# A depthwise convolution on VectorE: seven stored phases instead of four, and a layer norm two units later

## The chip, the cores and the metric

The kernel runs on one core of a Trainium2 chip. The metric is the device time of one execution in microseconds, from the start of the program to its end, taken over several runs of the same kernel; beside it stands one profiled execution, from which all the rows below come.

## The reference

A decoder trunk of two layers over 512 positions of 1024 channels (batch 1, float32). Layer 0 mixes tokens by a gated DeltaNet; layer 1, which the change touches, by a convolution module. Both layers then attend to a memory of 256 rows and apply a squared-ReLU MLP. The module of layer 1:

```python
def causal_depthwise_conv(x, w):
    """x (B, S, C), w (W, C); out[t] = sum_j w[j] * x[t - (W-1) + j] (left zero padding)."""

def conformer_conv(h, w_pw1, b_pw1, w_dw, b_dw, ln_g, ln_b, w_pw2, b_pw2):
    u = h @ w_pw1 + b_pw1
    u = u[..., :D_MODEL] * jax.nn.sigmoid(u[..., D_MODEL:])
    c = causal_depthwise_conv(u, w_dw) + b_dw
    c = jax.nn.silu(layer_norm(c, ln_g, ln_b))
    return c @ w_pw2 + b_pw2
```

The depthwise convolution has 31 taps per channel. Beside this module the kernel computes, in the same stage, the keys and values of layer 1's memory attention (`mem_h @ w_kv`), which depend on nothing in it.

## The kernel before

Activations lie transposed in SBUF: a tile is 128 channels by 512 positions, and 1024 channels are eight tiles, m = 0 to 7. In layer 1 the positions are kept in phases: column 128 r + i of a tile is position 4 i + r, so a tile is four phases of 128.

**Weights.** Every matrix arrives in half tiles of 128 x 1024. SyncE issues the load (`raw`, L193), ScalarE rounds it to the high half (`wh`, L204), VectorE subtracts for the low half (`wl`, L72), and each product is three matmuls: high by high, low by high, high by low (L220 to L222; L251 to L253 where the activation is the stationary side). The loads run up to four half tiles ahead, the splits three (`NW`). The third matmul of a unit is the first that needs `wl`.

**The stage.** `conformer` runs 32 units in the order of `CONV_SEQ`: 16 units "p" of the first projection (two for each channel tile, the value and the gate), then 16 units "k" of keys and values (eight for K, eight for V). After each unit, extra work is placed by hand in `CONV_AFTER`, as pairs of unit index and step:

- ("t", m): GpSimd builds the nine tap tiles of channel tile m (`taps`), for the convolution on TensorE.
- ("c", m, j...): convolution of column blocks j of tile m as matmuls with the tap tiles. Tiles 3 to 7 go this way; their gated input is first spread by 16 DMAs on SyncE into `xg`.
- ("d", m): for tiles 0 to 2 (`NDVE` is 3) the convolution is done on VectorE. "d" transposes the finished sum on TensorE (`cvT`) and adds it to the rows `cy` with their statistics.
- ("l", 0): layer norm over channels: aggregate, root, and eight normalisations on VectorE.
- ("o", m): transpose back, silu, and split of tile m, input to the final projection that follows unit 31.

**Taps on VectorE.** `pw_ev(m)` makes the gated input and, for m below 3, writes it into `xg`: four phases of 136 columns, of which the first 8 are zero. The tap with delay d, written as d = 4 u + e, adds to output phase r the input phase r - e shifted by u columns if r is at least e, and phase r + 4 - e shifted by u + 1 otherwise. So a tap with e = 0 is one instruction of 4 x 128 columns, and any other is two, of (4 - e) x 128 and e x 128 columns. The tap d = 0 runs on ScalarE and starts the sum `ca`. The tap instructions wait in a list, `todo`; after each unit and each convolution step `taps_dve(us)` issues `us * TAP_RATE` of them:

```python
            taps_dve(5.4 if kind == "p" else 2.8)
            for what, m, *js in after.pop(i, ()):
                {"t": taps, "c": lambda m: conv(m, js), "l": lambda m: ln(), "o": ln_out, "d": turn}[what](m)
                taps_dve({"c": 2.0 * len(js)}.get(what, 0.0))
```

The framework's scheduler orders the instructions of each engine and sets the semaphores; buffers come from pools and are reused in turn. The `cv` pool, from which `xg` comes, has six buffers for eight tiles; the `fs` pool has three buffers of 128 x 1024, which are otherwise used in layer 0 and at the very end.

Of the kernel before, what the change touches and what calls it, by code (L numbers as in the profile page):

```python
# [8 lines left out]
F32 = mybir.dt.float32  # L9
F32R = mybir.dt.float32r  # L10
AF = mybir.ActivationFunctionType
ALU = mybir.AluOpType
AX = mybir.AxisListType

P = 128
NT = 512
NDVE = 3
# [23 lines left out]
def tile_trunk(ctx, tc, xT, memT, prm_d, adt_d, bdw_d, w_ab, w_kq, w_v, w_z, w_dno, w_pw1, w_pw2,  # L41
               w_q, w_k, w_vv, w_o, w_up, w_dn, yT):
    nc = tc.nc
    pe, act, dve, pool = nc.tensor, nc.scalar, nc.vector, nc.gpsimd
# [3 lines left out]
    fsp = ctx.enter_context(tc.tile_pool(name="fsp", bufs=3))  # L48
# [6 lines left out]
    def nm(s):  # L55
        cnt[0] += 1
        return f"{s}_{cnt[0]}"

    def slot(dt=F32, s="u", shape=(P, NT)):
        return up.tile(list(shape), dt, tag="u", name=nm(s))  # L60
# [10 lines left out]
    def tt(e, o, a, b, op):  # L71
        e.tensor_tensor(out=o, in0=a, in1=b, op=op)  # L72

    def stt(o, a, s, b, op0, op1):
        dve.scalar_tensor_tensor(out=o, in0=a, scalar=s, in1=b, op0=op0, op1=op1)  # L75
# [7 lines left out]
    def c4(t):  # L83
        return t.rearrange("p (c i) -> p c i", c=4)
# [9 lines left out]
    def pc(name, i=0):  # L94
        return prm[:, OFF[name] + i:OFF[name] + i + 1]
# [67 lines left out]
    for kind, gq in DN_ORDER:  # L163
        for i in range(2):
            j = gq * 2 + i
            src = {"k": w_kq[gq * 4 + i], "q": w_kq[gq * 4 + 2 + i], "z": w_z[j], "v": w_v[j]}[kind]
# [781 lines left out]
    def conformer(norm, hres, nxt):  # L948
# [12 lines left out]
        def pw_ev(m):  # L961
            sg = slot(s="sg")
            tt(dve, sg, st.pop((m, 1)), norm.rb, ALU.mult)
            act.activation(sg, sg, AF.Sigmoid, bias=pc("b_pw1", 8 + m))
            a = slot(s="pa")
            tt(dve, a, st.pop((m, 0)), norm.rb, ALU.mult)
            x = wp.tile([P, 544], F32, tag="cv", name=nm("xg"), bufs=NCV)
            x4 = c4(x)
            pool.memset(x4[:, :, 0:8], 0.0)
            if m < NDVE:  # L970
                stt(x4[:, :, 8:136], c4(a), pc("b_pw1", m), c4(sg), ALU.add, ALU.mult)
                todo.extend(dve_conv(m, x4))
                return
            gl = slot(s="glu")
            stt(gl, a, pc("b_pw1", m), sg, ALU.add, ALU.mult)
            for j in range(4):
                for b in range(4):
                    nc.sync.dma_start(out=x4[32 * b:32 * b + 32, j, 8:136],
                                      in_=gl[32 * j:32 * j + 32, 128 * b:128 * b + 128])
            xg[m] = x4  # L980

        todo, acc = [], {}

        def dve_conv(m, x4):

            def tap(a, d, r0, r1, u):
                w = pc("w_tap", m * 31 + 30 - d)
                src = x4[:, (r0 - d) % 4:(r0 - d) % 4 + r1 - r0, 8 - u:136 - u]
                if d == 0:
                    act.activation(a[:, r0:r1, :], src, AF.Copy, scale=w)  # L990
                else:
                    stt(a[:, r0:r1, :], src, w, a[:, r0:r1, :], ALU.mult, ALU.add)

            acc[m] = slot(s="ca")
            for d in range(31):
                u, e = divmod(d, 4)
                yield lambda d=d, e=e, u=u: tap(c4(acc[m]), d, e, 4, u)
                if e:
                    yield lambda d=d, e=e, u=u: tap(c4(acc[m]), d, 0, e, u + 1)

        def taps_dve(us):
            for _ in range(min(len(todo), round(us * TAP_RATE))):
                todo.pop(0)()
# [60 lines left out]
        for i, (kind, u) in enumerate(CONV_SEQ):  # L1064
            if kind == "p":
                m, hf = divmod(u, 2)
                pw_mm(m, hf)
                if (m, hf) == (0, 0):
                    norm.stat()
                if (m, hf) == (1, 0):  # L1070
                    norm.spread()
                    pw_ev(0)
                if hf == 1 and m > 0:
                    pw_ev(m)
            else:
                kv_unit(1, u)
# [4 lines that stand above are left out]
# [84 lines left out]
    for gq in range(2):  # L1165
# [6 lines left out]
        for i in range(4):  # L1172
            h = 4 * gq + i
            m = MG[gq] + i * MSTEP[gq] // 2
# [34 lines left out]
    def do_w(m):  # L1209
        return wnext(("do", m // 2), m % 2), psum("do")  # L1210
# [11 lines left out]
    for m in range(2, 8):  # L1222
        w, ps = do_w(m)
# [52 lines left out]
    def out_half(half, prev):  # L1276
# [8 lines left out]
        for t in range(KT):  # L1285
# [3 lines left out]
            if t in OUT:  # L1289
# [30 lines left out]
REC = (39, 68)  # L1320
MEM = 53
MLP_ORDER = [("up", 0), ("up", 1), ("dn", 0), ("up", 2), ("dn", 1), ("up", 3), ("dn", 2), ("dn", 3)]
TAP_RATE = 1.5
CONV_SEQ = [("p", i) for i in range(16)] + [("k", i) for i in range(16)]
CONV_AFTER = [(3, ("t", 4)), (9, ("c", 3, 0, 1)), (11, ("c", 3, 2, 3)), (11, ("t", 5)), (12, ("c", 4, 0, 1)),
              (13, ("c", 4, 2, 3)), (13, ("t", 6)), (14, ("c", 5, 0, 1, 2, 3)), (14, ("t", 7)), (15, ("d", 0)),
              (16, ("c", 6, 0, 1, 2, 3)), (17, ("d", 1)), (18, ("c", 7, 0, 1, 2, 3)), (18, ("d", 2)), (18, ("l", 0))]
CONV_AFTER += [(23 + _m, ("o", _m)) for _m in range(8)]


def _tiles_a(np, w):
# [87 lines left out]
```

## Time and profile before

| | |
|---|---|
| median of 3 runs | 1600.11 us (1599.11 to 1601.5) |
| the profiled execution | 1601.85 us, of which the span of the program's instructions is 1599.7 |
| granted TensorE clock, mean | 0.983 of full speed |
| TensorE busy | 1542.7 us (96%) |
| VectorE busy | 924.3 us (58%) |
| ScalarE busy | 660.6 us (41%) |
| GpSimd busy | 275.9 us (17%) |
| chain that ended last | TensorE 89%, VectorE 3%, GpSimd 3%, ScalarE 2% |

Times in the profile are microseconds from the start of the span unless marked ns. A group of instructions is given by its line, engine, operation, and output and input tiles by the program's names, then the count, the busy time, the mean of one in ns, and the idle time of the engine before them with what ended it. Matmuls overlap, so a matmul's duration is longer than the distance between two starts; this holds in a small way for VectorE too.

### The profile page before, as it was taken

Reading aid. Unit: us, or ns where it says so; the run is one execution under the profiler, and the core shown is the slowest. Engines: PE = TensorE matmul, PEld = TensorE weight load, DVE = VectorE, ACT = ScalarE, POOL = GpSimd, SP = SyncE. Lnnn points to the kernel's source line nnn. Section 1 sums busy time; section 2 is a strip of 40 time slices with the busy share of each in tenths; the row PEclk is TensorE's granted clock in tenths of the full one; section 3 lists DMA queues with packets and bytes.
Section 4 is the critical chain, followed back from the end, with each engine's and each line's share of the span. In section 5 each row is a group of like instructions: output and inputs, shape, how many; then the busy total and the mean of one; then the engine's idle time right before and its main releaser. Section 6 shows DMA issues by size and latency. Waiting matters only on the chain.

```text
span 1599.7 us, 20039 instructions
## 1 busy us (share of the span) xinstructions
PE 1542.7 (96%) x7864; PEld 1307.5 (82%) x7864; DVE 924.3 (58%) x1373; ACT 660.6 (41%) x1011; POOL 275.9 (17%) x314
## 2 busy tenths in 40 slices
PE   9998997899999999999999999799999999999997
PEld 6777885798888888888888889788888888888897
DVE  6886878576455444343436599974545443444443
ACT  6656573745444433232314321173434442322332
POOL 1526334502111100000111308102012000000002
PEclk9999999899999999999999999899999999999999
DMA  5221112153211232232232421253213222322321
GB/s 178 67 72 60 53 51 95 53 172 110 94 63 64 92 105 93 94 104 92 94 104 93 141 90 47 85 160 106 79 40 99 95 97 92 105 93 93 104 93 53
DMA packets 47614, 147.09 MB, mean 92 GB/s; under 512 B 6304, under 2 KB 11040, under 8 KB 47520
## 3 DMA queue, kind: packets, MB, share of 16 engines
q1 hardware_dynamic: 47520, 145.81, 27.6%
q8 instruction: 62, 1.02, 0.3%
q14 instruction: 32, 0.26, 0.1%
HBM read 142.38 MB, written 2.10 MB: 90 GB/s over the span
## 4 chain that ended last, share of the span: by engine, by line
PE 89%; DVE 3%; POOL 3%; ACT 2%; issue 1%; DMA 0%; DVEq 0%; SPq 0%; POOLq 0%; ACTq 0%
PE dn L222 7%; PE dn L220 7%; PE dn L221 7%; PE up L220 7%; PE up L222 7%; PE up L221 7%; PE pw L220 3%; PE pw L221 3%; PE pw L222 3%; PE q L220 2%; PE xo L221 2%; PE q L221 2%; PE q L222 2%; PE cv L1024 2%; PE xo L220 2%; PE xo L222 2%
## 5 line engine op out<-in xcount | busy, mean ns | idle before, releaser
L204 ACT CAST wh<-raw 128x1024 fp32r<-128x1024 f32 x248 | 260.5, 1051 | 717.5 <-PE dn L221 191.4
L72 DVE TENSOR_TENSOR wl<-raw,wh 128x1024 fp32r<-128x1024 f32 x248 | 314.2, 1268 | 127.4 <-ACT wh L204 121.5
L220 PE MATMUL up<-xh,wh 128*128 128x512 f32 x512 | 200.2, 391 | 0.0
L222 PE MATMUL up<-xh,wl 128*128 128x512 f32 x512 | 199.2, 389 | 0.0
L221 PE MATMUL up<-xl,wh 128*128 128x512 f32 x512 | 199.2, 389 | 0.0
L220 PE MATMUL dn<-uh,wh 128*128 128x512 f32 x448 | 174.3, 389 | 0.0
L221 PE MATMUL dn<-ul,wh 128*128 128x512 f32 x448 | 174.3, 389 | 0.0
L222 PE MATMUL dn<-uh,wl 128*128 128x512 f32 x448 | 174.3, 389 | 0.0
L72 DVE TENSOR_TENSOR h<-dn,h 128x512 f32<-128x512 f32 x56 | 41.8, 747 | 170.4 <-PE dn L222 170.4
L75 DVE SCALAR_TENSOR_TENSOR rl<-up,rb 128x512 f32<-128x512 f32 x64 | 44.2, 691 | 156.9 <-PE up L222 156.9
L221 PEld LDWEIGHTS up<-xl,wh 128*128 128x128 f32 x512 | 96.1, 188 | 20.3 <-issue 0.5
L220 PEld LDWEIGHTS up<-xh,wh 128*128 128x128 f32 x512 | 96.1, 188 | 20.1 <-issue 0.5
L222 PEld LDWEIGHTS up<-xh,wl 128*128 128x128 f32 x512 | 96.1, 188 | 20.1
L72 POOL TENSOR_TENSOR tap<-ident,prm 128x512 f32<-128x512 f32 x45 | 61.0, 1388 | 278.6 <-PE up L222 263.8
L221 PEld LDWEIGHTS dn<-ul,wh 128*128 128x128 f32 x448 | 84.1, 188 | 17.6
L222 PEld LDWEIGHTS dn<-uh,wl 128*128 128x128 f32 x448 | 84.1, 188 | 17.5
L220 PEld LDWEIGHTS dn<-uh,wh 128*128 128x128 f32 x448 | 84.1, 188 | 17.3
L72 POOL TENSOR_TENSOR sq<-sq,sq 128x512 f32<-128x512 f32 x30 | 49.9, 1664 | 255.4 <-ACT sq L295 167.7
L75 DVE SCALAR_TENSOR_TENSOR ca<-xg,prm,ca 128x384 f32<-128x384 f32 (+3 forms) x159 | 88.2, 607 | 0.3
L220 PE MATMUL h<-xh,wh 128*128 128x512 f32 x192 | 77.5, 403 | 1.3 <-ACT xh L288 1.3
L221 PE MATMUL h<-xl,wh 128*128 128x512 f32 x192 | 75.5, 393 | 0.6 <-DVE xl L75 0.6
L222 PE MATMUL h<-xh,wl 128*128 128x512 f32 x192 | 75.2, 392 | 0.0
(320 smaller groups left out, 3204.4 us busy)
## 6 DMA issues: line engine op xcount, KB each, us to landing
raw<-w_up SPq DMA_DIRECT2D x64, 512.0 KB, 3.5
raw<-w_dn SPq DMA_DIRECT2D x64, 512.0 KB, 3.5
raw<-w_pw SPq DMA_DIRECT2D x24, 512.0 KB, 3.7
raw<-w_kq SPq DMA_DIRECT2D x16, 512.0 KB, 3.6
raw<-w_k SPq DMA_DIRECT2D x16, 512.0 KB, 3.7
raw<-w_vv SPq DMA_DIRECT2D x16, 512.0 KB, 4.0
raw<-w_q SPq DMA_DIRECT2D x16, 512.0 KB, 3.6
raw<-w_o SPq DMA_DIRECT2D x16, 512.0 KB, 3.6
```

Of the source, the lines that this page charges most:

```text
L72: e.tensor_tensor(out=o, in0=a, in1=b, op=op)
L75: dve.scalar_tensor_tensor(out=o, in0=a, scalar=s, in1=b, op0=op0, op1=op1)
L204: act.copy(h, raw)
L220: pe.matmul(ps, wh, xh, start=first, stop=False)
L221: pe.matmul(ps, wh, xl, start=False, stop=False)
L222: pe.matmul(ps, wl, xh, start=False, stop=last)
L1024: pe.matmul(o, x, TAPS[m][2 * j + u // 4][:, (u % 4) * P:(u % 4 + 1) * P], start=u == 0, stop=False)
```

## The change

For tiles 0 to 2 the gated input is now kept in seven phases of 144 columns in one `fs` buffer, `x7`. Phases 3 to 6 are the four phases as before, at column 8; phases 0 to 2 are copies of phases 4 to 6, shifted by one column, made by one ScalarE copy of 3 x 128 columns. Then output phases 0 to 3 of the tap (u, e) read the stored phases 3 - e to 6 - e, all with the same shift u, and every tap is one instruction of 4 x 128 columns. There are 93 tap instructions instead of 162, three of them on ScalarE as before. The zeros are 7 x 10 columns, set by GpSimd.

`TAP_RATE` goes from 1.5 to 0.75 instructions per microsecond of a step. The transposes of tile 2 and layer norm move from unit 18 to unit 20, and the eight outputs of layer norm each one unit later, the last now after unit 31. Tiles 3 to 7 keep their `xg` buffers.

```diff
--- before.py
+++ after.py
@@ -964,13 +964,16 @@
             act.activation(sg, sg, AF.Sigmoid, bias=pc("b_pw1", 8 + m))
             a = slot(s="pa")
             tt(dve, a, st.pop((m, 0)), norm.rb, ALU.mult)
+            if m < NDVE:
+                x7 = fsp.tile([P, 1024], F32, tag="fs", name=nm("x7"))[:, 0:1008].rearrange("p (q t) -> p q t", q=7)
+                pool.memset(x7[:, :, 0:10], 0.0)
+                stt(x7[:, 3:7, 8:136], c4(a), pc("b_pw1", m), c4(sg), ALU.add, ALU.mult)
+                act.copy(x7[:, 0:3, 9:137], x7[:, 4:7, 8:136])
+                todo.extend(dve_conv(m, x7))
+                return
             x = wp.tile([P, 544], F32, tag="cv", name=nm("xg"), bufs=NCV)
             x4 = c4(x)
             pool.memset(x4[:, :, 0:8], 0.0)
-            if m < NDVE:
-                stt(x4[:, :, 8:136], c4(a), pc("b_pw1", m), c4(sg), ALU.add, ALU.mult)
-                todo.extend(dve_conv(m, x4))
-                return
             gl = slot(s="glu")
             stt(gl, a, pc("b_pw1", m), sg, ALU.add, ALU.mult)
             for j in range(4):
@@ -981,22 +984,19 @@
 
         todo, acc = [], {}
 
-        def dve_conv(m, x4):
-
-            def tap(a, d, r0, r1, u):
-                w = pc("w_tap", m * 31 + 30 - d)
-                src = x4[:, (r0 - d) % 4:(r0 - d) % 4 + r1 - r0, 8 - u:136 - u]
+        def dve_conv(m, x7):
+
+            a = acc[m] = slot(s="ca")
+
+            def tap(d):
+                w, u, e = pc("w_tap", m * 31 + 30 - d), d // 4, d % 4
+                src = x7[:, 3 - e:7 - e, 8 - u:136 - u]
                 if d == 0:
-                    act.activation(a[:, r0:r1, :], src, AF.Copy, scale=w)
+                    act.activation(c4(a), src, AF.Copy, scale=w)
                 else:
-                    stt(a[:, r0:r1, :], src, w, a[:, r0:r1, :], ALU.mult, ALU.add)
-
-            acc[m] = slot(s="ca")
-            for d in range(31):
-                u, e = divmod(d, 4)
-                yield lambda d=d, e=e, u=u: tap(c4(acc[m]), d, e, 4, u)
-                if e:
-                    yield lambda d=d, e=e, u=u: tap(c4(acc[m]), d, 0, e, u + 1)
+                    stt(c4(a), src, w, c4(a), ALU.mult, ALU.add)
+
+            return [lambda d=d: tap(d) for d in range(31)]
 
         def taps_dve(us):
             for _ in range(min(len(todo), round(us * TAP_RATE))):
@@ -1320,12 +1320,12 @@
 REC = (39, 68)
 MEM = 53
 MLP_ORDER = [("up", 0), ("up", 1), ("dn", 0), ("up", 2), ("dn", 1), ("up", 3), ("dn", 2), ("dn", 3)]
-TAP_RATE = 1.5
+TAP_RATE = 0.75
 CONV_SEQ = [("p", i) for i in range(16)] + [("k", i) for i in range(16)]
 CONV_AFTER = [(3, ("t", 4)), (9, ("c", 3, 0, 1)), (11, ("c", 3, 2, 3)), (11, ("t", 5)), (12, ("c", 4, 0, 1)),
               (13, ("c", 4, 2, 3)), (13, ("t", 6)), (14, ("c", 5, 0, 1, 2, 3)), (14, ("t", 7)), (15, ("d", 0)),
-              (16, ("c", 6, 0, 1, 2, 3)), (17, ("d", 1)), (18, ("c", 7, 0, 1, 2, 3)), (18, ("d", 2)), (18, ("l", 0))]
-CONV_AFTER += [(23 + _m, ("o", _m)) for _m in range(8)]
+              (16, ("c", 6, 0, 1, 2, 3)), (17, ("d", 1)), (18, ("c", 7, 0, 1, 2, 3)), (20, ("d", 2)), (20, ("l", 0))]
+CONV_AFTER += [(24 + _m, ("o", _m)) for _m in range(8)]
 
 
 def _tiles_a(np, w):
```

## The prediction

> **What bounds the kernel now.** I read the page first (busy shares, slices, chain), then the stretches of 10 us around the conformer, then the groups by form, then the order in time of VectorE, GpSimd, SyncE and TensorE.
>
> ```profile
> span 1599.7 us, 20039 instructions
> PE 1542.7 (96%) x7864; PEld 1307.5 (82%) x7864; DVE 924.3 (58%) x1373; ACT 660.6 (41%) x1011; POOL 275.9 (17%) x314
> PE   9998997899999999999999999799999999999997
> DVE  6886878576455444343436599974545443444443
> PEclk9999999899999999999999999899999999999999
> ```
>
> TensorE is the bound nearly everywhere. Slices are 40 us wide; counted from 0, slice 25 (1000 to 1040 us) has TensorE at 7 and the clock at 8, while VectorE is at 9 in slices 23 to 25. That is the conformer. Cut finer (columns: PE, PEld, DVE, ACT, POOL busy, granted clock, DMA share, GB/s):
>
> ```profile
> 1000.00:1010.00 10.00, 10.00 (x91) 10.00 (x90) 9.93 (x22) 0.00 (x0) 4.15 (x4) 1.00 0.30 107
> 1010.00:1020.00 10.00, 1.27 (x11) 1.07 (x10) 9.93 (x23) 3.08 (x4) 0.00 (x0) 0.70 0.02 5
> 1020.00:1030.00 10.00, 7.03 (x43) 7.03 (x44) 10.00 (x29) 0.00 (x0) 0.00 (x0) 0.62 0.18 43
> ...
> 1010.44 0.60 PE L1008 MATMUL cvT<-ident,ca 128*128 128x128 f32 x4
> 1022.97 0.58 PE L222 MATMUL K<-mh,wl 128*128 128x256 f32 x1 [11.70 <-DVE wl L72]
> ...
> 1021.71 1.21 DVE L72 TENSOR_TENSOR wl<-raw,wh 128x1024 fp32r<-128x1024 f32 x1
> ```
>
> There is one stall in the conformer: 11.7 us before the third matmul of K unit 2. It waits for that unit's low half `wl`, a VectorE subtraction that starts at 1021.71, because VectorE, busy 9.93 us of every 10 here, is behind with its queue. So the stage's price is VectorE's queue ahead of this `wl`.
>
> **A second price, the clock.** After the stall TensorE is slow for a while. Third matmuls of neighbouring K triples, before and after it:
>
> ```profile
> 1008.51 0.28 PE L222 MATMUL K<-mh,wl 128*128 128x256 f32 x1
> 1008.87 0.28 PE L222 MATMUL K<-mh,wl 128*128 128x256 f32 x1
> ...
> 1023.78 0.41 PE L222 MATMUL K<-mh,wl 128*128 128x256 f32 x1
> 1024.42 0.41 PE L222 MATMUL K<-mh,wl 128*128 128x256 f32 x1
> ```
>
> A triple takes 0.64 us instead of 0.36; over seven triples that is 2.0 us. Stall and slow clock together: 13.7 us, the most that the change can win here. The Trainium skill (TensorE: Matmul & The Clock Gate, Part 1) says that the clock halves after an idle window of about 3.4 us and returns after as long a busy one; the granted 0.70 and 0.62 in the rows agree. By it, waits of 1 or 2 us, such as I expect below, leave the clock alone.
>
> **Fewer tap instructions.** Before, a tap whose shift is a multiple of four is one instruction of 512 columns; every other tap is two (384 and 128, or 256 twice). Where GpSimd rests:
>
> ```profile
> 910.40 0.74 DVE L75 SCALAR_TENSOR_TENSOR ca<-xg,prm,ca 128x512 f32<-128x512 f32 x1
> 911.06 0.74 DVE L75 SCALAR_TENSOR_TENSOR xg<-pa,prm,sg 128x512 f32<-128x512 f32 x1
> ...
> 921.27 0.87 DVE L75 SCALAR_TENSOR_TENSOR ca<-xg,prm,ca 128x384 f32<-128x384 f32 x2
> 922.06 0.74 DVE L75 SCALAR_TENSOR_TENSOR xg<-pa,prm,sg 128x512 f32<-128x512 f32 x1
> ```
>
> From start to start a single costs 0.66 us and a pair 0.79, so joining a pair saves 0.13. The new instruction reads four rows of 128 at a stride of 144 instead of 136; I take the single's 0.66 for it, since the shape is the same, and let its price vary in a rival.
>
> Now the queue. In the built order of VectorE, 145 tap instructions stand ahead of K unit 2's `wl` before (19 singles and 63 pairs): 19 x 0.66 + 63 x 0.79 = 62.3 us. In the changed order there are 77: 77 x 0.66 = 50.8 us. (TAP_RATE is halved, but 93 instructions come for 162, so part of the taps moves behind this point: 77 taps are done ahead of it instead of 82.) The rest of the queue ahead is the same. The queue is shorter by 11.5 us, so `wl` would end at 1022.92 - 11.5 = 1011.4, and TensorE is ready for it at about 1011.1 (the row of 1010.44, 0.44 us of transposes, two K matmuls at 0.12): 0.3 us of wait remain.
>
> **GpSimd's collisions.** Its tap tiles and VectorE's instructions with two SBUF operands get in each other's way:
>
> ```profile
> 958.47 24.49 POOL L72 TENSOR_TENSOR tap<-ident,prm 128x512 f32<-128x512 f32 x18
> 989.39 11.23 POOL L72 TENSOR_TENSOR tap<-ident,prm 128x512 f32<-128x512 f32 x6 [6.44 <-DVE glu L75]
> 1001.85 3.53 POOL L72 TENSOR_TENSOR tap<-ident,prm 128x512 f32<-128x512 f32 x3 [1.23 <-DMA xg<-glu]
> ...
> L969 POOL MEMSET xg<- 128x32 f32 x2 | 0.3, 126 | 56.1 <-DVE ca L75 41.3 <-PE cv L1027 14.9
> ...
> 960.01 1.33 DVE L75 SCALAR_TENSOR_TENSOR ca<-xg,prm,ca 128x512 f32<-128x512 f32 x1
> ...
> L75 DVE SCALAR_TENSOR_TENSOR ca<-xg,prm,ca 128x512 f32<-128x512 f32 x10 | 7.4, 741 | 0.0
> L75 DVE SCALAR_TENSOR_TENSOR ca<-xg,prm,ca 128x128 f32<-128x128 f32 x22 | 7.5, 343 | 0.0
> ...
> L75 DVE SCALAR_TENSOR_TENSOR ca<-xg,prm,ca 128x512 f32<-128x512 f32 x2 | 3.0, 1478 | 0.0
> L75 DVE SCALAR_TENSOR_TENSOR ca<-xg,prm,ca 128x128 f32<-128x128 f32 x2 | 2.3, 1131 | 0.0
> ```
>
> The first two groups are of 906 to 958 us, where GpSimd rests, the last two of 970 to 983, where it builds tiles: 741 becomes 1478 ns and 343 becomes 1131, about 0.8 us more, whatever the width. So a collision costs a fixed 0.8 us per instruction. In the order of time 24 such instructions lie beside the 27 tiles of these rows (18 + 6 + 3), the first at 960.01, the last at about 1004.5: 19 us together. The change leaves the tiles as they are, but not their times: GpSimd was held for 56.1 us in all by the memsets of two `xg` buffers (until 958), one of them still read by VectorE's first tap tile; the new tiles come from another pool, and in the built order all memsets stand far ahead. The 27 tiles start earlier, spread out by waits for the gated inputs, and by these waits all are still built ahead of K unit 2's `wl`. Bounds: all 27 collide, 2.4 us more; or a third of them find VectorE at an instruction that reads PSUM, some 6 us less, of which only 0.3 us could be used at this stall. I take +1.2.
>
> The Trainium skill (SBUF — State Buffer, section SBUF: two separate sides) says that the two engines lock the pair for a whole instruction and the loser stands still. A step that does not depend on width is what that gives, and it speaks against wider taps in one point: each tile of GpSimd then waits 0.66 instead of 0.26 to 0.53 for its turn. The rows have cover for that: the last tiles were done at 1005.4, and their matmuls begin at about 1014 in the forecast.
>
> **What is late next.** The queue is shorter ahead of K unit 2, but 13 taps are left behind it instead of 14 instructions: 13 x 0.66 = 8.6 us against 2 x 0.66 + 6 x 0.79 = 6.1, so 2.5 us more. Rows of the stretch behind it:
>
> ```profile
> 1048.03 2.35 DVE L72 TENSOR_TENSOR wl<-raw,wh 128x1024 fp32r<-128x1024 f32 x2
> ...
> 1051.24 0.39 PE L252 MATMUL V<-wl,mh 128*128 128x512 f32 x1
> ...
> 1017.44 10.45 SPq L978 DMA_DIRECT2D xg<-glu  x16
> ...
> DMA to landing us min/median/max: 1.7/1.8/4.8
> ...
> 1027.76 1.95 PE L1024 MATMUL cv<-tap,xg 128*128 128x128 f32 x16
> ...
> 1035.74 0.61 PE L1008 MATMUL cvT<-ident,ca 128*128 128x128 f32 x4
> ```
>
> (1) SyncE copies tile 7 of the gated input in 16 transfers, 10.45 us of issue, 2.6 per column block, each landing 1.8 later. They were issued around the stall. In the changed order `glu` of tile 7 stands 1.2 us of small instructions ahead of K unit 2's `wl`, so it ends at about 1009.0 and the blocks land at 1013.4, 1016.0, 1018.6 and 1021.2. TensorE finishes K unit 2 at 1014.0 and takes 2.0 us per block (8.0 for four): it waits 0.6 for the third and 0.6 for the fourth, 1.2 us. The weight load queued behind them on SyncE, issued from about 1019.5, is for K unit 5, which is reached (1014.0 + 8.0 + 1.2, two K units at 2.9) at about 1029.
>
> (2) The first V unit's `wl` (the first of the two at 1048.03) ended at 1049.24, 26.3 us after K unit 2's, with VectorE busy all that way; with the 2.5 it is 28.8. Layer norm (aggregates, root, eight normalisations) and the third tile's transposes lie inside that stretch in both orders, so their shift by two units costs nothing of its own. TensorE's way from K unit 2's third matmul to V's second, 1022.97 to 1051.24, is 28.3, less 2.0 of slow clock, plus the 1.2 of (1): 27.5. So it waits 1.3, and 0.5 more because layer norm's first four transposes now stand behind V's first two matmuls: 1.8 us.
>
> (3) The last of layer norm's outputs now follows the last V unit, with the final projection right behind. Its chain, and what hides it:
>
> ```profile
> L1057 ACT ACTIVATE la<-lnT,prm 128x512 f32<-128x512 f32 x8 | 6.2, 777 | 0.0
> L257 ACT CAST lsh<-la 128x512 fp32r<-128x512 f32 x8 | 5.0, 621 | 0.4
> L72 DVE TENSOR_TENSOR lsl<-la,lsh 128x512 fp32r<-128x512 f32 x8 | 5.5, 690 | 0.9 <-ACT lsh L257 0.6
> L257 ACT CAST Vh<-V 128x512 fp32r<-128x512 f32 x4 | 2.3, 582 | 0.3 <-PE V L253 0.3
> ...
> 943.74 0.39 PE L222 MATMUL pw<-xh,wl 128*128 128x512 f32 x1
> 944.43 0.40 PE L222 MATMUL pw<-xh,wl 128*128 128x512 f32 x1
> ```
>
> Silu 0.78, cast 0.62, subtraction 0.69, behind two casts of V at 0.58 and at most one weight split of about a microsecond on ScalarE: 4.3 us. The projection needs this tile for its last three of 24 matmuls; three take 0.69, so 21 take 4.8. Hidden, and if the cover fails it costs under 1 us.
>
> (4) Added: three copies of 384 columns on ScalarE (under 0.62 us each, the cast of 512) and wider memsets (0.13 for 32 columns each; 70 now). The copy lies between the gated tile and its first shifted tap; ScalarE idles there and VectorE does the next tile's multiplications meanwhile. If exposed, three times 0.6 us early in a queue that is then still short. Nothing taken.
>
> **Sum.** -13.7 + 0.3 + 1.2 (collisions) + 1.2 (transfers) + 1.8 (V unit) = -9.2 us. The profiled execution took 1601.85 us (its span of 1599.7 and 2.15 around it); 1592.6 for it. It lies 1.74 above the median of the runs, 1600.11, which I carry over: **1590.9 us**. This kernel's measurement can tell about 0.2% (3.2 us) from no change.
>
> **Rivals.** (A) The stall only moves. VectorE has hardly an idle moment between 906.8 and 1050, and everything behind it (K units 3 to 7, the V unit, the transfers) has 1 to 3 us of slack. If collisions cost 2.4 and the waits (1) and (2) double, the gain is 13.7 - 0.3 - 2.4 - 2.4 - 3.6 = 5.0: 1595. With a further 3 us of such waits it shrinks to 1598. For it: the slack is thin in each row. Against it: 11.5 us less work on the engine that is the bound there.
>
> (B) All is taken back: the time stays within 3 us of 1600. That would need another feeder of K unit 2, its weight load or cast, to be late as well; in the trace the cast's input had landed and only `wl` was waited for.
>
> (C) Slower. The joined instruction costs more than its like: its source has other strides, and it follows its forerunner on the same accumulator each time, with no short one between. It decides from 62.3 / 77 = 0.81 us on: there the queue is as long as before. At 0.95 us it is 73.2 - 62.3 = 10.9 us longer at K unit 2, and 13 x 0.95 - 6.1 = 6.3 longer behind it, of which the V unit's slack of 28.3 - 26.3 = 2.0 takes a part: 1600.1 + 10.9 + 4.3 = 1615. Against it: the 21 singles have the same shape, also wait for their forerunner, and take 0.66; nothing in the rows takes 0.8 alone.
>
> **How the numbers follow.** Forecast 0.65, with 1586.4 (all 13.7 won) to 1594 as its own range; (A) 0.20; (B) 0.05; (C) 0.10. The forecast's range and the greater part of (A), up to 1597, hold 8 in 10. Faster by over 0.2% (below 1596.9): the forecast, and 0.18 of (A), 0.83; within 0.2%: 0.02 of (A), (B), 0.07; slower 0.10.
>
> **What would show it.** Right: 90 tap groups `ca<-x7` of 512 columns at about 0.74 us alone and 1.48 beside GpSimd; tap tiles starting well before 958; the K matmul's idle time down from 11.7 to under 3 us; the granted clock near 1.00 from 1010 to 1030; small waits at the third and fourth block of tile 7 and before the first V unit; the final projection about 9 us earlier. Wrong: a K matmul still waiting over 5 us for `wl`, taps above 0.8 us, or new idle time on TensorE after 1014 that sums to more than 5 us.

## The result, and the profile after

The changed kernel takes 1595.34 us (median of 6 runs, 1593.49 to 1596.47) against 1601.22 us before (6 runs, 1599.11 to 1603.68): a ratio of 0.9961, 95% interval 0.9948 to 0.9974. In a second set of runs it took 1594.18 us (5 runs) against 1601.88, 0.9954 (0.9941 to 0.9966). So 6 to 8 us are gained where 9.2 were forecast. The profiled execution took 1596.47 us.

The page of after, the lines that answer to those of before:

```profile
span 1594.8 us, 19977 instructions
PE 1545.7 (97%) x7864; PEld 1310.7 (82%) x7864; DVE 919.2 (58%) x1304; ACT 661.9 (42%) x1014; POOL 275.3 (17%) x314
PE   9998997899999999999999999999999999999997
DVE  6886878566455444343445599974445443444443
PEclk9999999799999999999999999999999999999999
```

In slice 25 TensorE goes from 7 to 9 and the clock from 8 to 9; VectorE's total has hardly moved, 919 us for 924. Two of the stretches shown for before (PE, PEld, DVE, ACT, POOL busy, granted clock, DMA share, GB/s), and after them TensorE's and VectorE's rows in order of time around the stall:

```profile
1010.00:1020.00 10.00, 6.35 (x43) 6.14 (x42) 9.85 (x19) 3.08 (x4) 0.00 (x0) 0.85 0.05 13
1020.00:1030.00 10.00, 10.00 (x88) 10.00 (x88) 9.82 (x26) 0.57 (x1) 0.00 (x0) 0.98 0.39 119
...
1015.53 1.22 DVE L72 TENSOR_TENSOR wl<-raw,wh 128x1024 fp32r<-128x1024 f32 x1
...
1016.80 0.38 PE L222 MATMUL K<-mh,wl 128*128 128x256 f32 x1 [3.65 <-DVE wl L72]
1018.05 0.41 PE L222 MATMUL K<-mh,wl 128*128 128x256 f32 x1
1018.69 0.41 PE L222 MATMUL K<-mh,wl 128*128 128x256 f32 x1
1021.02 1.16 PE L1024 MATMUL cv<-tap,xg 128*128 128x128 f32 x9
...
1046.54 0.50 PE L252 MATMUL V<-wl,mh 128*128 128x512 f32 x1 [1.27 <-DVE wl L72]
```

The stall of K unit 2 is 3.65 us instead of 11.70, not gone: VectorE is still late with that `wl`. Behind the stall the triples again take 0.64 us (1018.05 to 1018.69). One small wait is left, 1.27 us before the first V unit. Now VectorE's taps in order of time, where GpSimd rests and then beside it, with GpSimd's first and last tap tiles and the group of all taps:

```profile
913.71 1.53 DVE L75 SCALAR_TENSOR_TENSOR ca<-x,prm,ca 128x512 f32<-128x512 f32 x2
915.16 1.22 DVE L72 TENSOR_TENSOR wl<-raw,wh 128x1024 fp32r<-128x1024 f32 x1
916.29 3.90 DVE L75 SCALAR_TENSOR_TENSOR ca<-x,prm,ca 128x512 f32<-128x512 f32 x5
920.11 0.68 DVE L72 TENSOR_TENSOR sg<-pw,rb 128x512 f32<-128x512 f32 x1
...
921.97 0.74 DVE L75 SCALAR_TENSOR_TENSOR ca<-x,prm,ca 128x512 f32<-128x512 f32 x1
922.63 0.74 DVE L75 SCALAR_TENSOR_TENSOR x<-pa,prm,sg 128x512 f32<-128x512 f32 x1
...
957.80 4.33 DVE L75 SCALAR_TENSOR_TENSOR ca<-x,prm,ca 128x512 f32<-128x512 f32 x3
962.06 0.68 DVE L72 TENSOR_TENSOR sg<-pw,rb 128x512 f32<-128x512 f32 x1
...
944.37 6.33 POOL L72 TENSOR_TENSOR tap<-ident,prm 128x512 f32<-128x512 f32 x4 [40.06 <-DVE glu L75]
...
1000.44 2.73 POOL L72 TENSOR_TENSOR tap<-ident,prm 128x512 f32<-128x512 f32 x2 [0.17 <-issue]
...
L75 DVE SCALAR_TENSOR_TENSOR ca<-x,prm,ca 128x512 f32<-128x512 f32 x90 | 81.8, 910 | 2.1
```

A tap with something else behind it starts 0.66 us ahead of its follower (921.97 to 922.63). Two taps in a row need 1.45 (913.71 to 915.16), five 3.82: each tap whose follower is the next tap of the same sum costs 0.79, not 0.66. That is what a *pair* of instructions cost before. Beside GpSimd three taps need 4.26 us, 1.42 each.

**One account for all runs.** In every trace I took the stretch from VectorE's first tap to the start of K unit 2's `wl` and divided the distance between starts by kind: what a tap of its width costs alone (0.263, 0.397, 0.529 and 0.662 us for 128 to 512 columns), what is above that by 0.06 to 0.3 us (a wait for the forerunner), what is above it by more (a collision with GpSimd), and everything else on VectorE. "Conformer" is from the first convolution matmul on TensorE to the first matmul of the final projection; the whole time also has in it what an execution did earlier, and the first convolution matmul lay anywhere from 937.4 to 942.4 us.

| kernel | taps ahead of `wl` | alone | forerunner | GpSimd | other work | first tap to `wl` | K stall | conformer | median, ratio to before |
|---|---|---|---|---|---|---|---|---|---|
| before | 145 | 62.5 | 0.7 | 15.5 | 35.6 | 114.28 | 11.70 | 136.9 | |
| after | 77 | 51.0 | 4.3 | 16.9 | 34.0 | 106.20 | 3.65 | 129.7 | 1595.34, 0.9961 |
| after, second set | 77 | 51.0 | 4.3 | 16.9 | 34.0 | 106.19 | 3.65 | 130.5 | 1594.18, 0.9954 |
| before's taps, after's places | 133 | 57.2 | 1.5 | 17.6 | 33.1 | 109.37 | 6.79 | 134.8 | 1600.14, 0.9984 |
| after's taps, before's places | 86 | 56.9 | 3.7 | 13.4 | 36.4 | 110.38 | 7.83 | 133.6 | 1597.90, 0.9971 |
| layer norm alone | 145 | 62.5 | 0.8 | 15.5 | 35.6 | 114.47 | 11.88 | 137.0 | 1600.53, 0.9994 |
| two sums, three tiles | 87 | 57.6 | 0.8 | 18.4 | 33.1 | 109.91 | 7.37 | 132.9 | 1597.91, 0.9973 |
| taps in halves | 148 | 58.8 | 0.2 | 17.0 | 33.1 | 108.89 | 6.34 | 135.2 | 1600.42, 0.9993 |
| two sums, two tiles | 78 | 51.6 | 1.2 | 16.4 | 33.9 | 103.14 | 0.59 | 126.9 | 1591.54, 0.9939 |
| tap tiles built for two channel tiles | 79 | 52.3 | 7.1 | 0.6 | 32.3 | 92.33 | 0 | 122.8 | 1586.88, 0.9909 |
| sum in PSUM | 72 | 47.7 | 6.0 | 5.8 | 33.1 | 92.39 | 0 | 122.7 | 1589.11, 0.9919 |

In the two rows with two sums the count has the two additions of the sums in it. In the last row the 5.8 us are nearly all VectorE waiting for its inputs, no collisions. In all nine rows with a stall, the stall is the seventh column less 102.5 to 102.6 us. TensorE's own way to that matmul is fixed; VectorE's queue sets the rest.

### The profile page after: what moved, and what is told of

Read it like the earlier page. It is cut to its first block, busy times and chain, and to the rows that moved or that the text cites. A ratio compares the mean times of both kernels' runs of the same rounds, so it can differ in the third digit from the quotient of the medians.

```text
span 1594.8 us, 19977 instructions
## 1 busy us (share of the span) xinstructions
PE 1545.7 (97%) x7864; PEld 1310.7 (82%) x7864; DVE 919.2 (58%) x1304; ACT 661.9 (42%) x1014; POOL 275.3 (17%) x314
## 4 chain that ended last, share of the span: by engine, by line
PE 83%; DVE 8%; ACT 3%; POOL 2%; issue 2%; SPq 1%; DMA 1%; DVEq 0%; ACTq 0%; POOLq 0%
PE dn L220 7%; PE dn L221 7%; PE dn L222 7%; PE up L220 7%; PE up L221 7%; PE up L222 7%; DVE ca L75 4%; PE q L220 2%; PE xo L221 2%; PE q L221 2%; PE q L222 2%; PE xo L222 2%; PE xo L220 2%; PE h L221 2%; PE pw L220 2%; PE pw L221 2%
## 5 line engine op out<-in xcount | busy, mean ns | idle before, releaser
L75 DVE SCALAR_TENSOR_TENSOR ca<-x,prm,ca 128x512 f32<-128x512 f32 x90 | 81.8, 910 | 2.1
```

## The experiments

**Place alone, join alone, layer norm alone.** The change has three parts. The first run gives the old taps the new places:

```diff
-TAP_RATE = 1.5
+TAP_RATE = 1.3
...
-              (16, ("c", 6, 0, 1, 2, 3)), (17, ("d", 1)), (18, ("c", 7, 0, 1, 2, 3)), (18, ("d", 2)), (18, ("l", 0))]
-CONV_AFTER += [(23 + _m, ("o", _m)) for _m in range(8)]
+              (16, ("c", 6, 0, 1, 2, 3)), (17, ("d", 1)), (18, ("c", 7, 0, 1, 2, 3)), (20, ("d", 2)), (20, ("l", 0))]
+CONV_AFTER += [(24 + _m, ("o", _m)) for _m in range(8)]
```

> The kernel before with only the places of after: its own taps (one or two instructions each, 153 in all) are issued at a rate of 1.3 instead of 1.5, which leaves the same share of them behind K unit 2 as in after, and layer norm comes two units later. Theory P (joining two halves that write different columns into one instruction that follows its forerunner on the same accumulator saves nothing back to back, 0.79 us for both; the gain of after is the 13 or so taps that now stand behind K unit 2's wl): that wl comes within 2 us of after's 1015.5, the stall of K unit 2 is 2 to 5 us, and the time is after's within 1.5 us, 1594 to 1597. Theory F (that of the forecast: a joined tap saves 0.13 us, so 53 to 57 pairs ahead of the wl cost some 7 us more than in after): stall about 10.5 us, 1600 to 1602, about the time before.

Measured 1600.14 us, 0.9984 (0.9975 to 0.9993); idle before the group of K's third matmuls:

```profile
L222 PE MATMUL K<-mh,wl 128*128 128x256 f32 x64 | 19.4, 303 | 7.0 <-DVE wl L72 7.0
```

The stall lies between the two, 6.8 us where P said 2 to 5 and F 10.5, and the time at the lower edge of F's range. Against after, the old taps cost 57.2 - 51.0 = 6.2 us more alone and 4.3 - 1.5 = 2.8 less in waiting for the forerunner. So joining saves about half of the 7 us of theory F, where theory P said nothing. The second run is the converse, TAP_RATE 0.85, layer norm at 18 and its outputs from 23 again in after:

> After with the places of before: the joined taps and the seven phases stay, but they are issued at 0.85 instead of 0.75, so that all are issued before K unit 2, and layer norm is at unit 18 and its outputs from 23 again. Theory P: nearly all of the gain goes, since 90 joined taps at 0.74 us on average take what 19 single ones and 63 pairs took (about 65 us against 62); stall of K unit 2 10 to 14 us, 1599 to 1603. Theory F: 90 taps at 0.66 (59 us) against 62 to 67 for the same 30 x 3 taps in pairs: stall 4 to 7 us, 1593 to 1597.

```profile
L222 PE MATMUL K<-mh,wl 128*128 128x256 f32 x64 | 19.0, 297 | 8.9 <-DVE wl L72 8.9
```

Measured 1597.90 us, 0.9971 (0.9959 to 0.9982); of the 8.9, 7.83 are at K unit 2 and 1.04 at a later K unit. Again between the two, the time just above F's. The conformer is 3.3 us shorter by the join alone and 2.1 by the place alone; together 7.2 (6.4 in the second set). Third, only layer norm moved in before, TAP_RATE at 1.5:

> The kernel before with only the third tile's transposes and layer norm two units later and its outputs one unit later; taps and their rate as before, so 145 tap instructions stand ahead of K unit 2's wl as before. Theory Q (the queue ahead of that wl sets the stall): the stall stays 11.7 us within 0.1 and the time is that of before within 1 us, 1600 to 1603. Rival L (layer norm's place pays by itself, since its aggregates and normalisations stood ahead of later low halves): at least 2 us faster, by less idle time after K unit 2.

```profile
L222 PE MATMUL K<-mh,wl 128*128 128x256 f32 x64 | 19.2, 300 | 11.9 <-DVE wl L72 11.9
```

1600.53 us, 0.9994 (0.9986 to 1.0003), stall 11.88: theory Q. Layer norm's shift is worth nothing by itself; whether the taps left behind K unit 2 need it was not tried.

**Is it the forerunner?** Two sums per tile, even taps in one and odd taps in the other, so that neighbours are independent:

```diff
+            a2 = wp.tile([P, 544], F32, tag="cv", name=nm("cb"), bufs=NCV)[:, 0:512]
...
+                if d == 31:
+                    tt(dve, a, a, a2, ALU.add)
+                    return
...
-                if d == 0:
-                    act.activation(c4(a), src, AF.Copy, scale=w)
+                t = a2 if d % 2 else a
+                if d < 2:
+                    act.activation(c4(t), src, AF.Copy, scale=w)
                 else:
-                    stt(c4(a), src, w, c4(a), ALU.mult, ALU.add)
+                    stt(c4(t), src, w, c4(t), ALU.mult, ALU.add)
```

> After with two accumulators for each of VectorE's tiles: even taps go to one, odd taps to the other (each started on ScalarE), so that no tap follows its forerunner on the same accumulator, and one addition at the end; the number of VectorE's instructions stays 90. Theory P (the 0.12 us between 0.79 and 0.67 is the wait for the forerunner's last write): taps start every 0.66 to 0.67 us where GpSimd is still, the queue ahead of K unit 2's wl is 5 to 8 us shorter, the stalls of K unit 2 (3.65) and of the first V unit (1.27) and the slow clock behind the first (about 1.6) go: 1588 to 1591. Rival S (the 0.79 us come from the width or the strides of the joined operands, or from the instruction's issue): still 0.79, no stall is shorter, 1594 to 1597.

VectorE in order of time, where GpSimd rests:

```profile
936.40 0.75 DVE L75 SCALAR_TENSOR_TENSOR ca<-x,prm,ca 128x512 f32<-128x512 f32 x1
937.07 0.75 DVE L75 SCALAR_TENSOR_TENSOR cb<-x,prm,cb 128x512 f32<-128x512 f32 x1
937.73 0.75 DVE L75 SCALAR_TENSOR_TENSOR ca<-x,prm,ca 128x512 f32<-128x512 f32 x1
938.39 0.75 DVE L75 SCALAR_TENSOR_TENSOR cb<-x,prm,cb 128x512 f32<-128x512 f32 x1
```

Same widths, same strides, 0.66 us apart: the 0.79 was the wait for the forerunner, and rival S falls. Yet the time is 1597.91 us, 0.9973 (0.9962 to 0.9984), worse than after, and the stall 7.37. The expectation took the queue's length from after; in the order that the scheduler now built, 87 instructions of the sums stand ahead of the `wl` instead of 77 (why it moved them is not shown), and the ten more (57.6 - 51.0 = 6.6 us) ate the 3.5 us saved. With two sums for tiles 0 and 1 only, the order keeps 78:

> Two accumulators for VectorE's tiles 0 and 1 only, one for tile 2; all else as after. In the built order 78 tap instructions stand ahead of K unit 2's wl (77 in after, 87 with two accumulators for all three). From the two-accumulator run: K unit 2's stall is the time from the first tap to that wl less 102.55 us in each of the six traces so far, and the waits for the forerunner fall from 4.3 us to 0.8. Theory P (that wait is the term that the forecast lacked): 78 x 0.66 = 51.6, waits about 1, collisions 17, other work 33 to 34: queue 103 to 104, stall 0.3 to 2; the first V unit's wait grows to 2 to 3 us since TensorE now comes there earlier; 1591 to 1594, 1.5 to 4 us under after. Rival S (two accumulators help nothing; the fuller queue of the run with three was the same cost in another place): stall 3 to 5, time within 1 us of after.

TensorE in order of time, then two stretches as above:

```profile
1011.07 0.38 PE L222 MATMUL K<-mh,wl 128*128 128x256 f32 x1 [0.59 <-DVE wl L72]
1013.81 1.95 PE L1030 MATMUL cv<-tap,xg 128*128 128x128 f32 x16
1016.31 2.02 PE L1030 MATMUL cv<-tap,xg 128*128 128x128 f32 x16 [0.39 <-DMA xg<-glu]
1020.96 2.02 PE L1030 MATMUL cv<-tap,xg 128*128 128x128 f32 x16 [0.40 <-DMA xg<-glu]
1041.02 0.50 PE L252 MATMUL V<-wl,mh 128*128 128x512 f32 x1 [1.47 <-DVE wl L72]
...
1010.00:1020.00 10.00, 9.02 (x78) 8.71 (x76) 9.75 (x20) 1.29 (x2) 0.00 (x0) 1.00 0.11 25
1020.00:1030.00 10.00, 9.60 (x83) 9.49 (x82) 8.97 (x24) 3.64 (x5) 0.00 (x0) 1.00 0.67 213
```

1591.54 us, 0.9939 (0.9925 to 0.9952), as theory P said (only the V unit waits less than the 2 to 3 us expected). This kernel is what the forecast described: stall 0.59, full clock, the transfers waited for twice (0.79 in all), the V unit 1.47, and within 0.7 us of the forecast's 1590.9. The converse splits every tap of after into two instructions of two rows:

> After with each tap split into two instructions of two rows each (180 instead of 90), all else in its place. Theory P: two halves write different columns, so neither waits for the other, and the pair costs 0.79 us, what the joined one costs back to back; where something stands between two joined taps (about a third of them, at 0.66) the split costs 0.12 us more, some 3 us on the queue: K unit 2's stall 4 to 8 us, 1595 to 1599. Theory F: splitting costs 0.13 us for each of 77 taps, 10 us: stall 13 to 14 us, 1604 to 1607.

```profile
913.26 2.85 DVE L75 SCALAR_TENSOR_TENSOR ca<-x,prm,ca 128x256 f32<-128x256 f32 x7
916.03 1.22 DVE L72 TENSOR_TENSOR wl<-raw,wh 128x1024 fp32r<-128x1024 f32 x1
...
L222 PE MATMUL K<-mh,wl 128*128 128x256 f32 x64 | 19.1, 299 | 7.7 <-DVE wl L72 7.7
```

Seven halves in 2.77 us, 0.396 each: no half waits, as each has one of other columns between itself and its forerunner. The stall (6.34) is P's; the time, 1600.42 us, 0.9993 (0.9984 to 1.0002), lies above P's range and below F's, for what the expectation left out: 32 halves behind the `wl` make the third tile's transposes, two K units and the V unit wait, 3.2 us together.

**GpSimd's share.** The largest term that the change left alone is the collisions. In the first run GpSimd builds no tap tiles for channel tiles 5 to 7, whose convolutions take tile 4's; so this kernel leaves out the right taps of three channel tiles. The trace has 18 builds in all instead of 45, and none of the 27 that after builds while VectorE's taps run; the expectation, which counts 18 of these 27 as gone, had that wrong.

> After with GpSimd building tap tiles only for channel tiles 3 and 4; the convolutions of tiles 5, 6 and 7 on TensorE use tile 4's. 79 taps ahead of K unit 2's wl. Leaves out the right taps of three channel tiles. Theory C (a collision costs a fixed 0.77 us; 22 of them, 16.9 us, stand ahead of the wl in after, and two thirds go with 18 of the 27 tiles): queue 106.2 + 1.3 (two taps more) - 8 to -12, so 96 to 100 against the 102.55 that TensorE needs: no stall at K unit 2, full clock, the V wait below 1: 1588 to 1591. Rival: the collisions only stretch instructions that would have waited for their forerunner or for data anyway: queue shorter by under 4 us, stall over 1, 1592 to 1595.

```profile
L75 DVE SCALAR_TENSOR_TENSOR ca<-x,prm,ca 128x512 f32<-128x512 f32 x90 | 67.4, 749 | 2.1
```

90 taps are busy 67.4 us instead of the 81.8 of after; 1586.88 us, 0.9909 (0.9896 to 0.9923), no TensorE wait over 0.15 us in the conformer. This is theory C, and more than it said: with all 27 builds gone the collisions fall from 16.9 to 0.6 us, the queue to 92.3 us instead of 96 to 100, and the time is 1.1 us under its range. The forerunner wait grows (7.1 us), since more taps stand in undisturbed runs, but only by 2.8: collisions and these waits overlap little. Then a version that keeps the work, with the sum in PSUM:

```diff
-    psp = ctx.enter_context(tc.tile_pool(name="psp", bufs=8, space=bass.MemoryType.PSUM))
+    psp = ctx.enter_context(tc.tile_pool(name="psp", bufs=7, space=bass.MemoryType.PSUM))
+    psa = ctx.enter_context(tc.tile_pool(name="psa", bufs=1, space=bass.MemoryType.PSUM))
...
-            a = acc[m] = slot(s="ca")
+            a = psa.tile([P, NT], F32, tag="psa", name=nm("cp"))
...
+            def out():
+                acc[m] = slot(s="ca")
+                act.copy(acc[m], a)
```

> After with the sum of VectorE's taps kept in PSUM (one bank of its own; the rotation for everything else has seven instead of eight) and copied to SBUF by ScalarE once per tile. 72 taps stand ahead of K unit 2's wl in the built order. In after, what VectorE reads from PSUM (pa, sg, cy) takes the same time beside GpSimd's tap tiles as alone, and what reads two SBUF operands (taps, wl) takes 0.7 to 0.85 us more. Theory C (the collision is of two engines at SBUF's operands, and one operand in PSUM ends it): no tap takes over 1.0 us beside GpSimd, the queue is 90 us or less, no stall at K unit 2 or V: 1586 to 1591 if seven banks suffice elsewhere; waits for a bank elsewhere, if they come, show as idle TensorE time outside the conformer, and may cost up to some 10 us. Rival D (the sum in PSUM comes back later, so that a tap waits longer for its forerunner): back-to-back taps over 0.85 us start to start, which from 1.1 us on eats the gain.

VectorE's and GpSimd's rows in order of time, and the two stretches:

```profile
946.42 1.42 DVE L73 TENSOR_TENSOR wl<-raw,wh 128x1024 fp32r<-128x1024 f32 x1
947.76 0.74 DVE L76 SCALAR_TENSOR_TENSOR cp<-x,prm,cp 128x512 f32<-128x512 f32 x1
...
968.97 6.29 DVE L76 SCALAR_TENSOR_TENSOR cp<-x,prm,cp 128x512 f32<-128x512 f32 x8
...
967.99 3.98 POOL L73 TENSOR_TENSOR tap<-ident,prm 128x512 f32<-128x512 f32 x3 [1.96 <-PE cv L1029]
972.74 2.06 POOL L73 TENSOR_TENSOR tap<-ident,prm 128x512 f32<-128x512 f32 x2 [0.76 <-DMA xg<-glu]
...
1010.00:1020.00 10.00, 10.00 (x89) 10.00 (x88) 8.80 (x23) 2.58 (x3) 0.00 (x0) 1.00 0.48 151
1020.00:1030.00 10.00, 10.00 (x88) 10.00 (x88) 8.93 (x18) 2.02 (x3) 0.00 (x0) 1.00 0.20 69
```

Eight taps in a row take 6.29 us, 0.79 each, with five of GpSimd's tiles beside them; in after a tap there took 1.42. In all, 31 taps of this run overlap a tile build, and the longest is recorded as 0.76 us. The `wl` of 946.42, two operands in SBUF, is still held (1.34 to the next start instead of 1.13). The queue is 92.4 us, a little over the 90 expected. Rival D falls: the wait for the forerunner is the same 0.12 to 0.13 in PSUM. TensorE waits nowhere in the conformer for more than 0.15 us. The time is 1589.11 us, 0.9919 (0.9907 to 0.9932), 5 us under after on the same chip: the fastest that computes all. The Trainium skill (SBUF — State Buffer, section SBUF: two separate sides) lists a VectorE operation with two SBUF inputs as one that contends with GpSimd; the rows agree, and show that the same tap with its sum, one input and the output, in PSUM does not.

What the eighth bank costs, in after alone:

> After with seven PSUM banks in the rotation instead of eight, and nothing else. In the run with the sum in PSUM TensorE's idle time before the conformer was 38.1 us against 35.3 to 35.7 in the other runs. Theory: that is the price of the eighth bank, so idle time before 900 us of 37.5 to 38.7 and a time 2 to 3 us above after, 1596 to 1597.5. Rival: the idle time there is that one execution's own, and the time is after's, 1594 to 1595.

```profile
76.33 0.79 PE L251 MATMUL z<-wh,xh 128*128 128x512 f32 x1 [1.95 <-DVE dt L72]
```

1597.74 us, 0.9976 (0.9967 to 0.9985), 2.4 to 3.5 us over after by the ratios to the two sets, and each of its 11 runs (1597.13 to 1600.26) lies above each of after's 11 (1592.88 to 1596.47), with the medians of before in the three sets 0.7 us apart at most. The wait of 1.95 at z is there as in the run with the sum in PSUM, but TensorE's idle time before 900 us sums to 32.9 us, not to 37.5 or more. So the price is real, and its place only partly found. Giving the bank up only from the conformer on (eight banks closed and seven and one opened ahead of it):

> The sum of the taps in PSUM as in the run with seven banks, but the rotation keeps its eight banks up to the conformer and gives one up only from there on. In the two runs with seven banks throughout, the first matmul of z waited 1.95 us instead of 0.45 and one of vt 0.77 instead of none, at 76 to 161 us. Theory: those 2.3 us come back and the conformer is as in the run before (no stall): 1586 to 1588. Rival: closing the eight banks and opening seven and one makes TensorE wait at the seam for all older tiles, and the gain is lost there (an idle stretch at about 900 us): 1589 to 1592.

```profile
885.95 0.47 PE L221 MATMUL pw<-xh,wh 128*128 128x512 f32 x1 [1.26 <-DVE h L73]
```

1590.08 us, 0.9922 (0.991 to 0.9935): no better. z waits 0.44 again, the seam costs 1.26; the rival holds in kind, at a lower price. Last, the same with before's four phases and places:

> The kernel before, its four phases, its one or two instructions per tap, its rate and layer norm's place, with only the sum of VectorE's taps in PSUM (a bank given up from the conformer on, one ScalarE copy per tile). In the built order 108 of the 159 tap instructions stand ahead of K unit 2's wl. Theory C (GpSimd's collisions, not the number of tap instructions, are the larger price: 15.5 us of the queue before against 11.5 us of free time between 145 and 77 instructions): no stall at K unit 2; taps moved behind it may make the first V unit or layer norm late by up to 4 us: 1587 to 1592, better than after. Rival N (the number of instructions decides, as the change has it): a stall of over 3 us somewhere in the conformer and 1594 or more.

TensorE's and ScalarE's rows:

```profile
1039.36 1.11 PE L1015 MATMUL cvT<-ident,ca 128*128 128x128 f32 x4 [14.31 <-ACT ca L1004]
...
1038.72 0.59 ACT L1004 COPY ca<-cp 128x512 f32<-128x512 f32 x1 [12.66 <-DVE cp L76]
```

1606.65 us, 1.0022 (1.0012 to 1.0032). K unit 2 does not wait, as C said, but C's time is missed by 15 us: the third tile's sum comes 14 us after its transposes, placed at unit 18, are reached. A stall of over 3 us and 1594 or more are the signs that rival N gave. They do not show N's reason: with one bank the three tiles run one after the other, and the places differ from after's too. Layer norm's place explains only a part: two K units are 5.75 us apart in the trace of before (third matmuls of units 3 and 5), and 8 to 9 of the 14.3 us would be left. VectorE's last tap starts at 1038.2 us here and at 1028.1 in the run with after's taps in PSUM. So the sum in PSUM did not make the kernel faster with the old taps in the old places, and what share the number of instructions, their order and the one bank have in that stays open; four phases with after's places and rate were not tried.

The changed kernel itself ran beside the run with two sums for two tiles, the one with fewer tap tiles and the first with the sum in PSUM:

> The changed kernel itself on the chip of the other runs: 1594 to 1597, a stall of 3.65 us at K unit 2 and of 1.3 at the first V unit again, to within 0.3 us, since the queue between first tap and wl is fixed work.

Stall 3.65 and V wait 0.83 instead of 1.27: the queue up to K unit 2 is the same to 0.01 us, as expected; what follows it is not, and the V wait lies 0.47 us off where 0.3 was allowed.

## Why the prediction came out as it did, step by step

**The bound** was right: one stall, set by VectorE's queue ahead of K unit 2's `wl`. The rule "stall = queue less 102.55" holds in all nine rows of the table that have one.

**Fewer tap instructions: right in count and in price alone, and short of one term.** 77 taps cost 51.0 us alone, as forecast (50.8), against 62.5 (62.3). What failed is the sentence "I take the single's 0.66 for it, since the shape is the same", with the defence that "the 21 singles have the same shape, also wait for their forerunner, and take 0.66". The singles quoted had another instruction behind them. The profile of before had it otherwise, in two rows in order of time that the prediction did not use:

```profile
951.74 0.75 DVE L75 SCALAR_TENSOR_TENSOR ca<-xg,prm,ca 128x512 f32<-128x512 f32 x1
952.52 0.62 DVE L75 SCALAR_TENSOR_TENSOR ca<-xg,prm,ca 128x384 f32<-128x384 f32 x1
```

0.78 apart, not 0.66: there the next tap reads columns that the single has just written. A pair hid this wait, because its two halves write different columns and each has the other between itself and its forerunner. The joined tap gives that cover up: 34 of the 77 wait, 4.3 us against 0.7 before. This term of +3.6 us is the miss. It is the mechanism of rival (C), which I had priced from 0.81 us per tap on and given one in ten; its real price, collisions aside, is (51.0 + 4.3) / 77 = 0.72 on average, because many taps have something else behind them.

**Collisions:** forecast +1.2 us, measured 16.9 - 15.5 = +1.4. The rest of the queue, taken to be the same, got 1.6 us shorter (35.6 to 34.0); why is not shown. Both together are 0.2 less than before. They started early, as said (944.37, not 958), and ended ahead of the `wl`. Together: -11.5 + 3.6 - 0.2 = -8.1 us, and the `wl` came 114.28 - 106.20 = 8.1 us earlier; 10.3 were forecast.

**The clock** was to be whole again. A stall of 3.65 us took it away once more: from the third K matmul of unit 2 to the convolution it is 4.22 us in after and 4.87 in its second profile, against 4.79 before and 2.74 in the run with a stall of 0.59. So 1.5 to 2.1 us were not won. The Trainium skill (TensorE: Matmul & The Clock Gate, Part 1) puts the idle window at about 3.4 us; 3.65 is just past it, the wait of 1.47 in the run with two sums for two tiles left the clock at 1.00 (1040 to 1050 us), and both agree.

**What is late next:** the waits for tile 7's transfers (1.2 forecast) did not come, since TensorE arrived later and slower; where it arrived on time, in the run with two sums for two tiles, they came at 0.39 and 0.40, at the second and fourth block. The V unit: 1.27 and 0.83, forecast 1.8. Layer norm's shift and its last output cost nothing, as said.

Summed from the forecast's -9.2: +2.15 at K unit 2 (3.65 for 1.5), +1.5 for the clock, -1.2 for the transfers, -0.5 at V gives -7.3; the conformer of the profiled execution is 7.2 shorter. The measured time lies where rival (A) put it, 1.3 us (second set: 0.2) above the forecast's own range of 1586.4 to 1594, but not by (A)'s mechanism: the stall did not move, it stayed. That the miss is no larger is in part luck: the 1.2 us forecast for the transfers were not spent only because TensorE came late.

Of the signs that the prediction named, two failed: K unit 2 waits 3.65 us, not under 3, and the clock from 1010 to 1030 is 0.85 and 0.98. The final projection starts 5.3 us earlier in the profiled execution (1076.17 to 1070.89; 7.2 by the conformer's length), not 9. The early tap tiles and the price beside GpSimd came as said.

## What to carry to other kernels

Read an instruction's price from start to start with the same kind of neighbour that it will have after the change: two that write different columns cover each other's wait for the forerunner, one joined instruction does not. Where an engine runs a chain on one sum, alternate two sums, and then look again at where the scheduler has put the chain, since the order can change with the chain: here 87 instructions instead of 77 came to stand ahead of what they delayed. And price what two engines do to each other beside the instructions themselves: here 15.5 us of collisions stood beside 11.5 us of saved instructions, and, with after's taps and places, a sum in PSUM ended nearly all of them.

## What the runs showed of the hardware

- VectorE's follower on the same tile waits 0.12 to 0.13 us for its forerunner (0.787 us for 0.662 at 512 columns), the same in SBUF and in PSUM; one independent instruction between them hides it all, even one of 128 columns.
- Beside GpSimd's tile builds a VectorE instruction with two SBUF operands (a tap) mostly takes 1.45 us to the next start instead of 0.66 to 0.79; with its sum (one input and the output) in PSUM it takes what it takes alone, 0.66 to 0.79.
- In the profiled executions with eight PSUM banks throughout the same code up to the conformer's first matmul took from 881.1 to 885.1 us, so a gain of a few us is read from one stage's length, not from the ends of two traces.
